# One 512-column matmul for the high weights with both parts of x, in a split-precision projection

## The chip, the cores and the metric

The kernel runs on one core of a Trainium2 chip. The metric is the device time of one execution in microseconds (us), the median of several. Engines are named as in the profile: PE is TensorE's matmul, PEld its weight load, DVE VectorE, ACT ScalarE, POOL GpSimd, SP SyncE, which issues nearly all DMAs.

## The reference

One layer on 256 tokens of width 2048, all in float32. Cut to what matters:

```
hn   = rms_norm(x, attn_norm_g)                      # (256, 2048)
proj = hn @ w_in                                     # 10656 columns
q, k, v      -> differential attention, 8 heads      # 3072 columns, "da"
r, k, v, 416 more columns -> RWKV-7, two scans       # 3488 columns, "rkv" and "lo"
gates = sigmoid(the last 4096 columns)               # "gt"
h = x + (gate_a * (y_a @ w_branch_a) + gate_b * (y_b @ w_branch_b)) @ w_out
out = h + expert_choice_ffn(rms_norm(h))             # 16 experts, 32 tokens each
```

The RWKV columns are mixed with their neighbours in time before use: p + mu * ((prev + next) / 2 - p).

## The kernel before, in words

Every projection of the first half is computed in a split form. A float32 operand a is taken as ah + al, where ah is a rounded to the type float32r and al is the rest; the product is xh·wh + xl·wh + xh·wl, three matmuls into one accumulator. `xh` and `xl` (lines 98 and 99) hold the normalised and transposed input for the whole kernel: 128 partitions, 16 slices of the contraction, 256 tokens. Lines 144 (ACT) and 145 (DVE) fill them.

`wsplit` (line 204) brings a **piece** of weights, 128 x 1024 numbers (512 KB), by one DMA into `raw`; ACT casts it into `wh` (line 211) and DVE subtracts to get `wl` (line 212). Both `wh` and `wl` have two buffers, so the cast of a piece waits until PE has done with the piece two before.

`project_c` (line 236) computes 256 output columns, transposed: two halves of 128 columns, each in its own accumulator (a bank of PSUM; the pool `pj` has two, so each half of the next projection needs the bank of the same half of this one). A projection takes four pieces; a piece serves four slices of the contraction for both halves, that is eight **triples** of matmuls of 256 columns on lines 249, 250 and 251. There are 30 such projections on w_in: 2 for the small RWKV inputs (`lo0`, `lo1`; the second half of `lo1` has 32 columns), 12 for r, k, v (`rkv`) and 16 for the gates (`gt`); with 2 x 16 triples each that makes 960 triples. Two more users of `project_c`, the branch projections (`br`), keep it. The attention inputs (`da`) and the output projection (`wo`) go through `project_t` (line 220), whose three matmuls have 512 columns.

What empties an accumulator before: for `gt`, one ACT activation (line 265) per half; for `rkv` and `lo`, `shift_mix` (line 293), an ACT copy into `prs` (line 296) and an ACT multiplication (line 300), then a POOL addition and a DVE combination.

Four groups of RWKV heads follow one another: `prep`, `invert` (a triangular inverse by 31 steps of small DVE operations, then four copies from PSUM per group, lines 533 to 544) and `chain` (the scan). The order of each engine's instructions is fixed at build time by a list scheduler with priorities: `prep`, `invert` and `chain` have a high one, so have the weights' cast and subtraction (`prio(PS)`) and the `rkv` mixing; the gates have a low one and fill in between (`GSCHED` deals 1, 4, 1, 4 and 6 of them to the groups). Each engine runs its own list strictly in that order.

After the gates come `da`, the attention, the two branch projections, `wo` with the router, and the experts, whose 384 loads of 1 MB of gate, up and down weights run by DMA to the end.

Of the kernel before, what the change touches and what calls it, by code (L numbers as in the profile page):

```python
# [8 lines left out]
F32 = mybir.dt.float32  # L9
F32R = mybir.dt.float32r  # L10
I32 = mybir.dt.int32
AF = mybir.ActivationFunctionType
OP = mybir.AluOpType
# [5 lines left out]
T = 256  # L19
KT = 16  # L20
DA_W = 1024
RW0 = 3 * DA_W
GATE0 = RW0 + 3488
# [29 lines left out]
def trunk_kernel(ctx, tc, x, attn_norm_g, w_in, q_norm_g, k_norm_g, lambda_q1, lambda_k1, lambda_q2,  # L53
# [4 lines left out]
    V, A, G, PE, SP = nc.vector, nc.scalar, nc.gpsimd, nc.tensor, nc.sync  # L58
# [39 lines left out]
    xh = hp.tile([128, KT, T], F32R, name="xh")  # L98
    xl = hp.tile([128, KT, T], F32R, name="xl")
# [117 lines left out]

    w_in_k = w_in[0].rearrange("(kt p) n -> p kt n", p=128)
# [40 lines left out]

    def gates(n):  # L260
        for gt in range(gates_done[0], min(16, gates_done[0] + n)):
            ps = project_c(w_in_k, KT, GATE0 + gt * 256, 256, xh, xl, f"gt{gt}")
            gs = wp.tile([128, 2, T], F32, name="gs", tag="gs", bufs=1)
            for c in range(2):
                A.activation(gs[:, c], ps[c], AF.Tanh, scale=0.5)
            SP.dma_start(gtD[2 * gt:2 * gt + 2].rearrange("c p t -> p c t"), gs)
            gates_done[0] += 1


    with ExitStack() as es:  # L270
# [22 lines left out]
        def shift_mix(ps, m, col, dst):  # L293
            pr = prs[prn[0] % 2]
            prn[0] += 1
            A.copy(pr[:m, 1:T + 1], ps)
            s = r2.tile([128, T], F32, name="shs")
            b = r2.tile([128, T], F32, name="shb")
            last_mix[0] = G.tensor_tensor(s[:m], pr[:m, 0:T], pr[:m, 2:T + 2], op=OP.add)
            A.mul(b[:m], ps, omu[:m, col:col + 1])  # L300
            V.scalar_tensor_tensor(dst, s[:m], prmh[:m, col:col + 1], b[:m], op0=OP.mult, op1=OP.add)
# [31 lines left out]
        ps = project_c(w_in_k, KT, RW0 + 3072, 256, xh, xl, "lo0")  # L333
# [6 lines left out]
        ps = project_c(w_in_k, KT, RW0 + 3328, 160, xh, xl, "lo1")  # L340
# [151 lines left out]
        def invert(G_):  # L492
# [39 lines left out]
            for a_, b_ in ab_:  # L532
                V.tensor_copy(ht[b_], ph[b_])
# [8 lines left out]
            for a_, b_ in ab_:  # L542
                V.tensor_copy(tt[a_, :, 0:4, 32:64], px[a_])
                V.tensor_copy(tt[b_, :, 4:8, 0:32], px[b_])
# [88 lines left out]
        for gp in range(4):  # L633
            rkv = []
            for i in range(3):
                ps = project_c(w_in_k, KT, RW0 + i * 1024 + gp * 256, 256, xh, xl, f"rkv{gp}_{i}")
# [425 lines left out]
```

## Time and profile before

| what | value |
|---|---|
| median of 3 runs | 1839.66 us (1839.43 to 1848.39) |
| the profiled execution's own time | 1838.98 us |
| its span, first to last instruction | 1836.9 us |
| granted TensorE clock, mean | 0.990 of 2.4 GHz |
| PE busy | 1652.7 us (90%), 11083 matmuls |
| DVE, ACT, POOL busy | 701.4, 440.2, 199.2 us |
| DMA queue 1 | 554.41 MB, 81.1% of 16 engines |

The span lies within one execution; 2.1 us more lie around it. Busy times are sums over engine instructions. A matmul's duration includes its way through the array and overlaps the next one's, so the spacing of starts, not the duration, tells how fast a stream of matmuls runs. By stage: up to about 552 us `lo`, `rkv`, `gt` and the RWKV groups; up to 680 us `da`; attention and branches up to 826 us; `wo` and router up to 920 us; experts to the end.

### The profile page before, as it was taken

The page shows a single profiled execution, that of the slowest core. Times are in us where ns is not written, and L with a number is a line of the kernel's source. Part 1 is how long each engine was busy: PE and PEld are TensorE (multiplying, and loading weights), DVE is VectorE, ACT ScalarE, POOL GpSimd, SP SyncE. Part 2 cuts the span into 40 slices and gives each one's busy share as a digit, 9 for nine tenths or more (in the row PEclk, how much of TensorE's full clock was granted, in tenths as well). Part 3 has the DMA queues.
Part 4 walks back from the last instruction along what each step waited for, and adds up shares of the span by engine and source line. Part 5 has one row for each costly group of instructions (what it writes and reads, how often), then busy time and mean ns, then how long its engine had stood idle before and what let it go on. Part 6 is the DMA issues. An engine that isn't in the chain of part 4 may idle for free.

```text
span 1836.9 us, 27260 instructions
## 1 busy us (share of the span) xinstructions
PE 1652.7 (90%) x11083; PEld 1012.1 (55%) x11083; DVE 701.4 (38%) x1520; ACT 440.2 (24%) x766; POOL 199.2 (11%) x308
## 2 busy tenths in 40 slices
PE   6999999999999999999888898888988879888887
PEld 5988988888998778998633332112521115221122
DVE  4687878787746777774410010000100001000001
ACT  5434444443434455444300000000000000000000
POOL 3243223333001321000000000000000000000000
PEclk9999999999999999999989999999999999999999
DMA  6555644456656666789799999999999999999998
GB/s 184 164 141 152 169 120 127 120 139 154 175 141 181 195 209 204 225 271 363 294 390 427 423 420 426 427 427 424 421 425 427 427 425 420 425 426 427 426 420 358
DMA packets 222141, 556.47 MB, mean 303 GB/s; under 512 B 40154, under 2 KB 129104, under 8 KB 188992
## 3 DMA queue, kind: packets, MB, share of 16 engines
q1 hardware_dynamic: 221440, 554.41, 81.1%
q8 instruction: 87, 1.43, 0.3%
q0 software_dynamic: 576, 0.31, 0.2%
q14 instruction: 38, 0.31, 0.1%
HBM read 543.14 MB, written 11.53 MB: 302 GB/s over the span
## 4 chain that ended last, share of the span: by engine, by line
DMA 45%; PE 40%; DVE 7%; POOL 3%; issue 2%; SPq 1%; ACT 1%; DVEq 0%; POOLq 0%; ACTq 0%
DMA w<-in_w_gate_e_dram 22%; DMA w<-in_w_down_e_dram 13%; DMA w<-in_w_up_e_dram 9%; PE pd L982 2%; PE pc_gt L251 2%; PE pc_gt L249 2%; PE pc_gt L250 2%; PE pxe L933 2%; PE pj_da L231 2%; PE pj_da L232 2%; PE pj_da L233 2%; PE pc_rkv L249 2%; PE pc_br L249 2%; PE pc_rkv L251 2%; PE pc_rkv L250 2%
## 5 line engine op out<-in xcount | busy, mean ns | idle before, releaser
L951 PE MATMUL pgu<-w,xe 128*32 128x512 f32 x2048 | 473.9, 600 | 86.4 <-DMA w<-in_w_up_e_dram 44.6
L951 PEld LDWEIGHTS pgu<-w,xe 128*32 128x32 f32 x2048 | 113.7, 109 | 439.8 <-issue 207.3
L982 PE MATMUL pd<-w,hdT 128*32 128x512 f32 x1024 | 217.1, 598 | 32.7 <-DMA w<-in_w_down_e_dram 31.8
L968 DVE SCALAR_TENSOR_TENSOR th<-th,pgu 128x512 f32<-128x512 f32 x8 | 5.5, 688 | 469.4 <-ACT th L967 416.4
L982 PEld LDWEIGHTS pd<-w,hdT 128*32 128x32 f32 x1024 | 54.0, 109 | 182.7 <-issue 90.4
L249 PE MATMUL pc_gt<-xh,wh_gt 128*128 128x256 f32 x512 | 149.1, 294 | 0.0
L251 PE MATMUL pc_gt<-xh,wl_gt 128*128 128x256 f32 x512 | 143.7, 292 | 3.8 <-DVE wl_gt L212 3.5
L250 PE MATMUL pc_gt<-xl,wh_gt 128*128 128x256 f32 x512 | 145.2, 286 | 0.0
L967 ACT ACTIVATE th<-pgu 128x512 f32<-128x512 f32 x8 | 4.8, 598 | 489.8 <-PE pgu L951 489.8
L249 PE MATMUL pc_rkv<-xh,wh_rkv 128*128 128x256 f32 x384 | 112.5, 295 | 2.8 <-ACT shb L300 1.8
L251 PE MATMUL pc_rkv<-xh,wl_rkv 128*128 128x256 f32 x384 | 110.4, 298 | 2.1 <-DVE wl_rkv L212 2.1
L250 PE MATMUL pc_rkv<-xl,wh_rkv 128*128 128x256 f32 x384 | 111.3, 292 | 0.0
L249 PEld LDWEIGHTS pc_gt<-xh,wh_gt 128*128 128x128 f32 x512 | 98.3, 192 | 3.2 <-issue 1.2
L251 PEld LDWEIGHTS pc_gt<-xh,wl_gt 128*128 128x128 f32 x512 | 95.7, 192 | 7.2 <-DVE wl_gt L212 4.8
L250 PEld LDWEIGHTS pc_gt<-xl,wh_gt 128*128 128x128 f32 x512 | 98.5, 192 | 2.0 <-issue 1.3
L212 DVE TENSOR_TENSOR wl_gt<-raw_gt,wh_gt 128x1024 fp32r<-128x1024 f32 x64 | 80.1, 1251 | 31.1 <-ACT wh_gt L211 27.8
L211 ACT CAST wh_gt<-raw_gt 128x1024 fp32r<-128x1024 f32 x64 | 66.9, 1046 | 78.9 <-PE pc_gt L250 64.4
L992 DVE TENSOR_TENSOR acc<-poe,acc 128x512 f32<-128x512 f32 x24 | 16.6, 692 | 175.9 <-PE poe L991 175.9
L987 ACT COPY ye<-pd 128x512 f32<-128x512 f32 x16 | 9.4, 586 | 301.1 <-PE pd L982 301.1
L249 PEld LDWEIGHTS pc_rkv<-xh,wh_rkv 128*128 128x128 f32 x384 | 75.3, 196 | 6.2 <-ACT shb L300 2.6
L232 PE MATMUL pj_da<-wl_da,xh 128*128 128x512 f32 x192 | 76.6, 399 | 1.7 <-DVE wl_da L212 1.7
L251 PEld LDWEIGHTS pc_rkv<-xh,wl_rkv 128*128 128x128 f32 x384 | 73.5, 196 | 5.1 <-DVE wl_rkv L212 2.8
(398 smaller groups left out, 2789.1 us busy)
## 6 DMA issues: line engine op xcount, KB each, us to landing
w<-in_w_gate_e_dram SPq DMA_DIRECT2D x128, 1024.0 KB, 19.6
w<-in_w_up_e_dram SPq DMA_DIRECT2D x128, 1024.0 KB, 19.6
w<-in_w_down_e_dram SPq DMA_DIRECT2D x128, 1024.0 KB, 18.2
raw_gt<-in_w_in_dram SPq DMA_DIRECT2D x64, 512.0 KB, 3.8
raw_rkv<-in_w_in_dram SPq DMA_DIRECT2D x48, 512.0 KB, 3.8
raw_da<-in_w_in_dram SPq DMA_DIRECT2D x48, 512.0 KB, 3.6
raw_wo<-in_w_out_dram SPq DMA_DIRECT2D x32, 512.0 KB, 6.7
raw_br<-in_w_branch_b_dram SPq DMA_DIRECT2D x16, 512.0 KB, 4.7
```

The lines of the kernel that those rows point to most:

```text
L211: cast_ = A.copy(wh[:, :n], raw[:, :n])
L212: low_ = V.tensor_tensor(wl[:, :n], raw[:, :n], wh[:, :n].bitcast(F32), op=OP.subtract)
L231: PE.matmul(ps[t], lh[:, kt, s], wh[:, j], start=first, stop=False)
L232: PE.matmul(ps[t], lh[:, kt, s], wl[:, j], start=False, stop=False)
L233: PE.matmul(ps[t], ll[:, kt, s], wh[:, j], start=False, stop=last)
L249: PE.matmul(ps[c][:m], wh[:, j, cs], rh[:, kt], start=first, stop=False)
L250: PE.matmul(ps[c][:m], wh[:, j, cs], rl[:, kt], start=False, stop=False)
L251: PE.matmul(ps[c][:m], wl[:, j, cs], rh[:, kt], start=False, stop=last)
L933: PE.matmul(px[:, j], h[:, t, kt::KT], ohr[:, t], start=t == 0, stop=t == 1)
L951: PE.matmul(pgu[2 * gu + hf][js], xe[kt // 4][:, kt % 4, js], wt[j][:, k, hf * 512:(hf + 1) * 512], start=kt == 0, stop=kt == KT - 1)
L982: mm = PE.matmul(pd[nb][js], hT[:, ft, js], wf[j], start=ft == 0, stop=ft == 7)
L992: V.tensor_tensor(acc[:, t, cs], po, (h if q == 0 else acc)[:, t, cs], op=OP.add)
```

## The change

`xh` and `xl` become two halves of one tile, side by side for each slice of the contraction. A new `project_w` replaces `project_c` for the 30 projections on w_in: one matmul of 512 columns multiplies the high weights with both (`high`), its result filling a whole bank, xh·wh in the first 256 columns and xl·wh in the last; a matmul of 256 columns adds xh·wl to the first half (`low`). The last slice of a projection runs low before high. A new helper `both` adds the two halves of the bank: ACT copies the second into SBUF, DVE adds the first to it. For the gates the activation then runs once on 512 columns in SBUF; in `shift_mix`, ACT's multiplication reads the sum instead of PSUM. Four copies per group in `invert` go from DVE to ACT.

```diff
-    xh = hp.tile([128, KT, T], F32R, name="xh")
-    xl = hp.tile([128, KT, T], F32R, name="xl")
+    xx_ = hp.tile([128, KT, 2, T], F32R, name="xx_")
+    xh, xl = xx_[:, :, 0], xx_[:, :, 1]
...
+    def project_w(c0, width, name):
+        nct = (width + 127) // 128
+        ps = [pjp.tile([128, 2, T], F32, name=f"pc_{name}_{c}", tag="pj") for c in range(nct)]
+        for kc in range(KT // 4):
+            wh, wl = wsplit(w_in_k[:, 4 * kc:4 * kc + 4, c0:c0 + width], 4, width, f"{name}_{kc}")
+            for c in range(nct):
+                m = min(128, width - c * 128)
+                for j in range(4):
+                    kt = 4 * kc + j
+                    cs = slice(c * 128, c * 128 + m)
+                    high = lambda: PE.matmul(ps[c][:m].rearrange("p a t -> p (a t)"), wh[:, j, cs],
+                                             xx_[:, kt].rearrange("p a t -> p (a t)"), start=kt == 0, stop=kt == KT - 1)
+                    low = lambda: PE.matmul(ps[c][:m, 0], wl[:, j, cs], xh[:, kt], start=False, stop=False)
+                    for f in (high, low) if kt < KT - 1 else (low, high):
+                        f()
+        return ps
...
+    def both(dst, ps):
+        A.copy(dst, ps[:, 1])
+        V.tensor_tensor(dst, ps[:, 0], dst, op=OP.add)
...
-            ps = project_c(w_in_k, KT, GATE0 + gt * 256, 256, xh, xl, f"gt{gt}")
+            ps = project_w(GATE0 + gt * 256, 256, f"gt{gt}")
...
-                A.activation(gs[:, c], ps[c], AF.Tanh, scale=0.5)
+                both(gs[:, c], ps[c])
+            A.activation(gs, gs, AF.Tanh, scale=0.5)
...
-            A.copy(pr[:m, 1:T + 1], ps)
+            both(pr[:m, 1:T + 1], ps)
...
-            A.mul(b[:m], ps, omu[:m, col:col + 1])
+            A.mul(b[:m], pr[:m, 1:T + 1], omu[:m, col:col + 1])
...
-                V.tensor_copy(ht[b_], ph[b_])
+                A.copy(ht[b_], ph[b_])
...
-                V.tensor_copy(tt[a_, :, 0:4, 32:64], px[a_])
-                V.tensor_copy(tt[b_, :, 4:8, 0:32], px[b_])
+                A.copy(tt[a_, :, 0:4, 32:64], px[a_])
+                A.copy(tt[b_, :, 4:8, 0:32], px[b_])
```

The order of instructions moves where one gate projection follows another. The first place is PE's list where the gate projection `pc_gt_..5920` takes over from the one before it (in the name `pc_gt_0` and `pc_gt_1` are the halves, in `wh_gt_0` and `wh_gt_1` the pieces). Before, from the end of piece 0 in the first half:

```order
L251 MATMUL pc_gt_0_5920<-xh,wl_gt_0_5924 128x256
L249 MATMUL pc_gt_0_5920<-xh,wh_gt_1_5953 128x256
L250 MATMUL pc_gt_0_5920<-xl,wh_gt_1_5953 128x256
L249 MATMUL pc_gt_1_5921<-xh,wh_gt_0_5923 128x256
L250 MATMUL pc_gt_1_5921<-xl,wh_gt_0_5923 128x256
L251 MATMUL pc_gt_1_5921<-xh,wl_gt_0_5924 128x256
```

The same place in the changed kernel, whose tile there is `pc_gt_..5930`:

```order
L232 MATMUL pc_gt_0_5930<-xx__82,wl_gt_0_5934 128x256
L230 MATMUL pc_gt_0_5930<-xx__82,wh_gt_1_5955 128x512
L232 MATMUL pc_gt_0_5930<-xx__82,wl_gt_1_5956 128x256
...
L232 MATMUL pc_gt_0_5930<-xx__82,wl_gt_1_5956 128x256
L230 MATMUL pc_gt_1_5931<-xx__82,wh_gt_0_5933 128x512
L232 MATMUL pc_gt_1_5931<-xx__82,wl_gt_0_5934 128x256
```

The second half's first piece, which stood behind one slice's two `wh` products of piece 1, now stands behind all four pairs of piece 1 in the first half, those with `wl` of piece 1 among them. That three or four of these `wl` products stand ahead of the second half's first piece is so at 14 of the 29 changes from one projection to the next, and was at none; with other PE work between at some.

The second place is DVE's list at the same change of projection, in the changed kernel (`wl_gt_1_5956` is the subtraction for the new projection's piece 1, `gs<-pc_gt_1_5834` the added sum that frees the second half's bank of the old one; `tmp`, `xx`, `hng` belong to `invert` and `chain`):

```order
L212 TENSOR_TENSOR wl_gt_1_5956<-raw_gt_1_5954,wh_gt_1_5955 128x1024
L535 TENSOR_TENSOR tmp<-xx,dd 128x16x2
L94 SCALAR_TENSOR_TENSOR hngr<-hng_t,hngr 128x8
L282 TENSOR_TENSOR gs<-pc_gt_1_5834,gs 128x256
L537 TENSOR_TENSOR xx<-xx,tmp 128x16x2
```

The bank is freed behind the subtraction. Before, DVE had no part in freeing it.

The third place is ACT's list there. Before (`gs<-pc_gt` empties the old projection's halves):

```order
L211 CAST wh_gt_0_5923<-raw_gt_0_5922 128x1024
L265 ACTIVATE gs<-pc_gt_0_5794 128x256
L211 CAST wh_gt_1_5953<-raw_gt_1_5952 128x1024
L265 ACTIVATE gs<-pc_gt_1_5795 128x256
```

and in the changed kernel:

```order
L211 CAST wh_gt_0_5933<-raw_gt_0_5932 128x1024
L281 COPY gs<-pc_gt_0_5833 128x256
L211 CAST wh_gt_1_5955<-raw_gt_1_5954 128x1024
L281 COPY gs<-pc_gt_1_5834 128x256
```

ACT's part stands where it stood: the second half's copy comes behind the cast of piece 1.

## Rows read from the trace of the kernel before

**Rows 1.** The page: busy time, and the span in 40 slices of 46 us.

```profile
PE 1652.7 (90%) x11083; PEld 1012.1 (55%) x11083; DVE 701.4 (38%) x1520; ACT 440.2 (24%) x766; POOL 199.2 (11%) x308
...
PE   6999999999999999999888898888988879888887
...
DVE  4687878787746777774410010000100001000001
...
GB/s 184 164 141 152 169 120 127 120 139 154 175 141 181 195 209 204 225 271 363 294 390 427 423 420 426 427 427 424 421 425 427 427 425 420 425 426 427 426 420 358
```

**Rows 2.** Stretches: PE, PEld, DVE, ACT, POOL busy (x instructions), clock, DMA share, GB/s.

```profile
92.00:138.00 46.00, 43.23 (x460) 40.18 (x459) 37.23 (x64) 18.23 (x29) 20.55 (x24) 1.00 0.50 140
184.00:230.00 46.00, 45.17 (x587) 41.47 (x586) 40.58 (x91) 19.67 (x35) 10.77 (x15) 1.00 0.63 167
506.00:552.00 46.00, 46.00 (x533) 42.03 (x532) 18.99 (x25) 17.60 (x30) 4.04 (x8) 1.00 0.48 138
827.00:873.00 46.00, 46.00 (x221) 37.02 (x221) 21.54 (x20) 21.05 (x28) 1.41 (x8) 1.00 0.99 363
```

**Rows 3.** The page: the chain that ended last, share of the span by engine.

```profile
DMA 45%; PE 40%; DVE 7%; POOL 3%; issue 2%; SPq 1%; ACT 1%; DVEq 0%; POOLq 0%; ACTq 0%
```

**Rows 4.** PE's groups by line and shape: count, busy us, mean ns, idle before.

```profile
L249 PE MATMUL pc_gt<-xh,wh_gt 128*128 128x256 f32 x512 | 149.1, 294 | 0.0
...
L249 PE MATMUL pc_rkv<-xh,wh_rkv 128*128 128x256 f32 x384 | 112.5, 295 | 2.8 <-ACT shb L300 1.8 <-ACT wh_rkv L211 0.9
...
L249 PE MATMUL pc_lo<-xh,wh_lo 128*128 128x256 f32 x48 | 14.1, 303 | 0.3 <-ACT xh L144 0.3
...
L249 PE MATMUL pc_lo<-xh,wh_lo 128*32 128x256 f32 x16 | 4.5, 279 | 0.0
```

**Rows 5.** Timeline of PE, gates: two starts, 12 matmuls of 256 columns apart.

```profile
500.11 0.28 PE L251 MATMUL pc_gt<-xh,wl_gt 128*128 128x256 f32 x1
...
501.55 0.28 PE L251 MATMUL pc_gt<-xh,wl_gt 128*128 128x256 f32 x1
```

**Rows 6.** Timeline of PE, `da`: two starts, 7 matmuls of 512 columns apart.

```profile
599.76 0.39 PE L232 MATMUL pj_da<-wl_da,xh 128*128 128x512 f32 x1
...
601.35 0.39 PE L233 MATMUL pj_da<-wh_da,xl 128*128 128x512 f32 x1
```

**Rows 7.** Groups of DVE and ACT by shape: count, busy us, mean ns, idle before.

```profile
L533 DVE COPY ht<-ph 32x512 f32<-32x512 f32 x8 | 5.5, 690 | 2.0 <-PE ph L529 1.9
...
L544 DVE COPY tt<-px 32x256 f32<-32x256 f32 x8 | 3.4, 424 | 0.3
...
L471 DVE TENSOR_TENSOR z<-pz,rkv 128x256 f32<-128x256 f32 x8 | 3.3, 410 | 0.0
...
L265 ACT ACTIVATE gs<-pc_gt 128x256 f32<-128x256 f32 x32 | 12.2, 381 | 14.2 <-PE pc_gt L251 14.0
...
L296 ACT COPY prs<-pc_rkv 128x256 f32<-128x256 f32 x24 | 8.9, 371 | 18.6 <-PE pc_rkv L251 18.6
...
L730 ACT ACTIVATE sqq<-qs 128x512 f32<-128x512 f32 x8 | 5.1, 633 | 0.3
...
L848 ACT COPY hT<-pth 128x512 f32<-128x512 f32 x8 | 4.4, 586 | 0.0
```

**Rows 8.** Timeline, one gate projection taking over from another at 485.08 us.

```profile
484.08 0.38 ACT L265 ACTIVATE gs<-pc_gt 128x256 f32<-128x256 f32 x1 [0.75 <-PE pc_gt L251]
...
485.08 0.28 PE L249 MATMUL pc_gt<-xh,wh_gt 128*128 128x256 f32 x1
485.17 1.05 ACT L211 CAST wh_gt<-raw_gt 128x1024 fp32r<-128x1024 f32 x1 [0.70 <-PE pc_gt L250]
...
486.12 0.38 ACT L265 ACTIVATE gs<-pc_gt 128x256 f32<-128x256 f32 x1
...
486.24 1.23 DVE L212 TENSOR_TENSOR wl_gt<-raw_gt,wh_gt 128x1024 fp32r<-128x1024 f32 x1 [0.79 <-ACT wh_gt L211]
```

**Rows 9.** Who PE waited for up to 560 us: us in total, times, longest.

```profile
PE pprg L116 <- DMA rowg<-in_attn_norm_g_dram: 12.9, 1, 12.9
PE pz L470 <- DVE X L464: 5.0, 3, 1.8
PE pc_gt L251 <- DVE wl_gt L212: 3.5, 4, 1.0
```

More of the change, by code (lines that the diff above doesn't have):

```diff
@@ L332, in trunk_kernel @@
         tc.cur_priority = keep_
-        ps = project_c(w_in_k, KT, RW0 + 3072, 256, xh, xl, "lo0")
+        ps = project_w(RW0 + 3072, 256, "lo0")
         for i, dst in enumerate((thw, adw)):
@@ L339, in trunk_kernel @@
             A.activation(dst[64:128, 1], tl_[64:128], fn)
-        ps = project_c(w_in_k, KT, RW0 + 3328, 160, xh, xl, "lo1")
+        ps = project_w(RW0 + 3328, 160, "lo1")
         for i, m in enumerate((128, 32)):
@@ L635, in trunk_kernel @@
             for i in range(3):
-                ps = project_c(w_in_k, KT, RW0 + i * 1024 + gp * 256, 256, xh, xl, f"rkv{gp}_{i}")
+                ps = project_w(RW0 + i * 1024 + gp * 256, 256, f"rkv{gp}_{i}")
                 dst = r2.tile([128, 2, T], F32, name=f"rkv_{i}", bufs=1)
```

## The prediction

> **What bounds the kernel now.** I read the page first. PE is busy in nearly every slice, DVE is busy to seven or eight tenths in the first dozen slices and hardly at all from the twentieth on, and the transfer rate stands at about 425 GB/s from slice 22 to the end [rows 1]. So there are two halves. The experts are bound by DMA, as the chain of waits says with its 45% for DMA [rows 3]; their first loads fill the DMA engines from about 827 us [rows 2], the last row, so that whatever is won or lost before that point moves the end by the same amount. The change lies wholly in the first 552 us.
>
> The stretches show what rules there [rows 2]. PE is busy for 43 to 46 of 46 us, DVE for 37 to 41 in the stretches with the inverse and for 19 near the end of the gates. The table of waits finds little else: after the 12.9 us of the start, PE's longest sums are 5.0 and 3.5 us [rows 9]. PE is the first bound, DVE a close second between 92 and 414 us. Gates and `rkv` projections are the filler that PE always has, so a shorter filler shortens the stage, unless PE is made to wait.
>
> **What a triple costs, and a pair.** The groups count 512 + 384 + 48 + 16 = 960 triples on w_in [rows 4]. Their means of 279 to 303 ns contain the way through the array, so I take the spacing of starts. Twelve matmuls of 256 columns take 501.55 - 500.11 = 1.44 us, 0.120 us each [rows 5]; seven of 512 take 601.35 - 599.76 = 1.59 us, 0.227 us each [rows 6]. The columns streamed are the same 768 either way; what goes is one fixed share per instruction, 2 x 0.120 - 0.227 = 0.013 us. A triple of 0.360 becomes a pair of 0.347, and 960 of them save 960 x 0.013 = **12.4 us** (with the unrounded 0.0129). No row shows a 512 followed by a 256. At worst the pair costs what the triple does, 0 us saved; at best the 256 hides its fixed share as well, another 0.013 us, 24.8 us saved in all. I take the sum of the two spacings, since each is measured in a stream of its own with a weight load per matmul.
>
> Here a page speaks against the change. The rows make the share that goes 13 ns. The Trainium skill, "TensorE: Matmul & The Clock Gate", section "Back-to-back issue gap", gives columns divided by 2.4 GHz plus 2.5 ns as the isolated spacing: 109 and 216 ns, so that 2.5 ns per triple would go, 2.4 us in all as an estimate. The trace does not agree (120 and 227 ns), and I go by it.
>
> **What emptying a bank costs.** Each of 60 halves gets a DVE addition of a bank's 256 columns and SBUF, 0.410 us by the nearest row, 24.6 us. In return 8 copies of 0.690 and 16 of about 0.42 leave DVE, 12.2 us [rows 7]. DVE has 12.4 us more, in a stage where it has 5 to 9 us to spare in each stretch of 46 [rows 2]: beside PE's work on average, not at every place. ACT: 32 gate activations of 0.381 become 32 copies of 0.371 and 16 activations of 0.633; with the moved copies (8 of at most 0.586, 16 of about 0.37) it has some 20 us more [rows 7], hidden, since it is busy for 18 to 20 us of 46 [rows 2]. The multiplication in `shift_mix` now waits for the sum, which delays `prep` by about half a microsecond per half: it stands behind a whole projection of 11 us for the next operand, and I cost it at nothing; without that cover it would be 24 x 0.4 = 10 us.
>
> Now the path. A bank was free 0.38 us after ACT took it up; now it is ACT's copy and then DVE's addition, 0.371 + 0.410 and some 0.1 us between, about 0.9 us if both are idle. PE needs the first half's bank when the second half has had its last four pairs, 1.39 us later, so a change of projection without other work just fits. At the first change (`lo0` to `lo1`) and where DVE is late it does not; I put **1.5 us** in all, from 0 to 6.
>
> The larger item is the order. One clean change of projection stands in the trace: the next projection starts at 485.08, the cast of its piece 1 at 485.17 (both buffers were taken until then), ACT empties the second half only at 486.12 behind that cast, and the subtraction ends at 486.24 + 1.23 = 487.47, 2.39 us after the start [rows 8]. Before, PE came to that `wl` late, behind both halves of piece 0. In the changed kernel the second half's bank is freed behind cast, copy, subtraction and addition, about 2.9 us after the start, so the scheduler has put piece 1 of the first half ahead of piece 0 of the second, at 14 changes (the order of PE, DVE and ACT above). The first `wl` of piece 1 is then due 4 x 0.347 + 0.227 = 1.62 us after the start; it is there at 2.39, or 2.5, as the last matmul has 512 columns and ends 0.11 us later. PE waits 0.85 us. At five of the 14 nothing else stands between; at the others other PE work covers 0.03 to all of it, which I counted from the order with the spacings above. The sum is **7.5 us**. There is a second wait behind it: the buffer of piece 0 is held until the second half is done with it, and then PE has only piece 1's four pairs and two of piece 2's highs, 1.39 + 0.45 = 1.84 us, until it needs piece 2's `wl`, 2.45 us away: 0.6 us, left whole at three changes and in parts at others, **2.5 us**. If other DVE work delays these subtractions by half a microsecond each time, both grow to 17 us together; if the chain's work that runs on meanwhile saves PE later waits, half of it comes back.
>
> **The sum**, against the profiled execution: 1838.98 - 12.4 + 7.5 + 2.5 + 1.5 = 1838.1, rounded to **1838.0 us**. The median of the three runs shown is 1839.66, 0.7 us above that execution; a difference of 0.5%, 9.2 us, is about what a measurement of this kernel can tell from no change, so below 1830.5 is faster and above 1848.9 slower. The forecast is no difference that can be told.
>
> **The rivals.**
> *The saving arrives.* PE waits at the changes of projection, but the RWKV groups' work runs on then and PE finds its later operands ready; or the 512 gives back more. For it: PE's waits are few before [rows 9], and DVE is busy only 19 of 46 us in the last gates [rows 2], where four of the 14 changes lie. Against it: an in-order PE that waits for `wl` in a stretch of nothing but filler gets nothing back. With 2 us of waits left it gives 1838.98 - 12.4 + 2 = 1828.6 us, faster.
>
> *DVE becomes the bound.* Its place is 92 to 414 us, where it has as little as 5.4 us to spare of 46 [rows 2]. It gets 12.4 us more there, subtractions come later, and the banks hang on it too. The point from which it decides: when the additions find DVE busy so often that its 12.4 us add to the stage, while the waits above grow to 17 us. The time: 1838.98 - 12.4 + 12.4 + 11.5 = 1850.5 us with the waits as summed, up to 1856 with the grown ones, slower. Against it: DVE waits for others too, and idle time between is used by a list scheduler.
>
> *The pair costs as much as the triple.* The columns are the same 768; if the weight load of the 512 cannot hide under the shorter 256, nothing is saved. Then only the waits are left: 1838.98 + 11.5 = 1850.5 us with all of them, 1842 if a third. Against it: weight loads hide at a spacing of 0.120 us now [rows 5]. By the page's 2.5 ns, the saving would be 2.4 us and the time 1848, an estimate near this case; the trace's two spacings speak against that as well.
>
> **How the numbers follow.** The forecast, waits that eat most of the saving, gets 0.50; the saving arrives 0.24; DVE the bound 0.16; pair as triple 0.10, half of it slower and half within. That makes faster 0.25 (with a hundredth from the forecast's lower edge), same 0.54, slower 0.21. The forecast's own range is 1831 to 1846, from a half to one and a half times the 11.5 us of waits and the smaller unknowns. To leave out no more than 2 in 10 it must take in most of the first two rivals: 1827 to 1851 us.
>
> **What would show it.** Right: in the changed profile, starts of pairs 0.347 us apart in a gate stretch; `da` starts within a few microseconds of before; PE's table of waits has new entries at the low matmuls (waiting for DVE's subtraction `wl_gt`, some 5 to 15 us) and the high ones (for the added halves), and the lines of the experts are unchanged. Wrong in size: pairs 0.36 apart (the third rival), or no such waits (the first). Wrong in kind: DVE busy for over 43 of 46 us in the stretches from 92 to 414 us with PE waiting for `prep` and `chain` operands (the second), or a difference that comes after 827 us, which nothing here foresees.

## The result, and the profile after

The changed kernel takes 1852.79 us (median of 7 runs, 1851.10 to 1855.18), the kernel before 1842.18 us (7 runs, 1839.43 to 1848.39): a ratio of 1.0051, 95% interval 1.0038 to 1.0063. It is slower by 10.6 us; the forecast was 1838.0 us, with a range from 1827 to 1851. The profiled executions differ by more, 1851.1 against 1836.9 us of span, since that of before (1838.98 us) lay 3.2 us under its median. The page of the changed kernel, busy time and slices, beside [rows 1]:

```profile
PE 1656.4 (89%) x10123; PEld 951.8 (51%) x10123; DVE 710.3 (38%) x1556; ACT 461.1 (25%) x806; POOL 197.3 (11%) x308
...
PE   6998999989999999999979898888988889888887
...
DVE  4678878797746677875420010000100001000001
...
PEclk9999999999999999999989999999999999999999
```

960 matmuls are gone and PE's busy time has not fallen; DVE has 9 us more. The chain that ended last, beside [rows 3], tells nothing of it:

```profile
DMA 46%; PE 39%; DVE 7%; POOL 2%; issue 2%; SPq 2%; ACT 1%; DVEq 0%; ACTq 0%; POOLq 0%
```

First, where. The first matmul of the branches starts at 710.2 us before and 723.8 after; `wo`, the experts and the end follow 13.9 to 14.2 us later than before. So all of it lies ahead of the branches, and behind them nothing changed, as predicted. The stretches, first those of [rows 2] in the changed kernel:

```profile
92.00:138.00 46.00, 42.85 (x303) 34.54 (x302) 34.48 (x63) 19.19 (x30) 17.25 (x21) 0.96 0.49 141
184.00:230.00 46.00, 41.56 (x412) 33.94 (x413) 39.07 (x88) 22.90 (x40) 12.54 (x16) 1.00 0.60 164
506.00:552.00 46.00, 43.87 (x514) 35.72 (x513) 19.21 (x25) 23.09 (x44) 4.97 (x8) 1.00 0.61 165
827.00:873.00 46.00, 46.00 (x230) 38.25 (x229) 23.81 (x24) 20.22 (x24) 1.22 (x7) 1.00 0.91 328
```

In the first two, DVE is no busier than it was (34.5 and 39.1 us, before 37.2 and 40.6), but PE is idle for 4.4 us of 46 in the second, where it was idle for 0.8. Now three long stretches (the same columns), the kernel before:

```profile
46.00:552.00 506.00, 483.15 (x5423) 446.52 (x5421) 381.25 (x837) 215.81 (x377) 135.87 (x185) 0.99 0.54 145
552.00:598.00 46.00, 44.86 (x209) 36.78 (x208) 29.67 (x60) 19.98 (x23) 8.75 (x14) 1.00 0.62 183
```

and the changed one:

```profile
46.00:552.00 506.00, 469.21 (x4384) 381.23 (x4383) 382.54 (x862) 232.76 (x411) 133.93 (x185) 0.98 0.53 142
552.00:598.00 46.00, 45.48 (x288) 36.39 (x287) 27.05 (x55) 19.36 (x24) 0.00 (x0) 1.00 0.55 161
```

PE was idle for 506 - 483.15 = 22.9 us between 46 and 552, and is for 36.8: **13.9 us more**. The granted clock fell to its lower level five times up to the branches, and does eight times, 3.41 us each (each fall takes 0.04 off the clock of a stretch of 46 us); half of that is lost, 8.5 us before and 13.6 after: **5.1 us more**. That holds for these two executions. Over the executions on record with their clock, its mean is 0.9886 for the kernel before (87 of them, from 0.985 at some 1846 us to 0.993 at 1839) and 0.9874 for the change (7), a difference of some 2 us: part of the 5.1 is the spread between executions.

Whom PE waits for, 46 to 552 us (in total, times, longest), beside [rows 9]:

```profile
PE pc_gt L232 <- DVE wl_gt L212: 6.7, 9, 2.3
PE psn L621 <- DVE uu L617: 4.4, 2, 3.3
PE pc_gt L230 <- DVE prs L282: 3.9, 1, 3.9
PE ph L554 <- DVE tst L544: 3.3, 2, 2.5
...
PE pc_gt L230 <- DVE gs L282: 2.7, 3, 1.7
PE pc_rkv L232 <- DVE wl_rkv L212: 2.2, 2, 1.8
PE pc_gt L230 <- DVE pp__4524 L447: 2.0, 1, 2.0
```

Added up over the whole list: low matmuls 9.6 us (before, L251: 5.8), high ones 10.3 (before, L249 and L250: 2.7; of the 10.3, 7.6 are waits for the added halves, `prs` and `gs`), the RWKV groups' products 16.3 (before 13.9). One place shows the new wait and what it draws after it. DVE, then ACT, then PE:

```profile
149.89 1.21 DVE L212 TENSOR_TENSOR wl_gt<-raw_gt,wh_gt 128x1024 fp32r<-128x1024 f32 x1
157.98 0.22 DVE L535 TENSOR_TENSOR tmp<-xx,dd 128x62 f32<-128x62 f32 x1 [6.89 <-DMA dd<-scn]
...
158.89 0.42 DVE L282 TENSOR_TENSOR prs<-pc_rkv,prs 128x256 f32<-128x256 f32 x1
```
```profile
152.71 0.37 ACT L281 COPY prs<-pc_rkv 128x256 f32<-128x256 f32 x1 [0.53 <-PE pc_rkv L230]
152.98 1.05 ACT L211 CAST wh_gt<-raw_gt 128x1024 fp32r<-128x1024 f32 x1
159.35 0.51 ACT L325 ACTIVATE shb<-prs,omu 128x256 f32<-128x256 f32 x1 [5.32 <-DVE prs L282]
```
```profile
159.37 0.79 PE L230 MATMUL pc_gt<-xx__82,wh_gt 128*128 128x512 f32 x1 [3.86 <-DVE prs L282]
...
160.17 0.63 PE L230 MATMUL pc_gt<-xx__82,wh_gt 128*128 128x512 f32 x1
160.60 0.41 PE L232 MATMUL pc_gt<-xx__82,wl_gt 128*128 128x256 f32 x1
160.81 0.63 PE L230 MATMUL pc_gt<-xx__82,wh_gt 128*128 128x512 f32 x1
```

ACT had copied its halves of both banks by 153.1 us. The addition stands in DVE's list behind the inverse's first step, and that waits 6.89 us for its DMA, with DVE idle. The bank stays taken, PE stands for 3.86 us, ACT's multiplication for 5.32. Then the clock is at its lower level, and pairs run 0.64 us apart instead of 0.35. Two stretches there show it; the clock is the number behind the five engines:

```profile
155.50:159.10 3.60, 0.01 (x1) 0.00 (x0) 1.01 (x5) 0.00 (x0) 0.00 (x0) 0.99 1.05 287
159.10:162.50 3.40, 3.13 (x9) 2.67 (x10) 3.30 (x8) 2.83 (x8) 1.88 (x3) 0.51 0.03 11
```

DVE's waits for that DMA in all (up to 560 us), before and in the changed kernel:

```profile
DVE tmp L510 <- DMA dd<-scn: 15.3, 4, 5.6
```
```profile
DVE tmp L535 <- DMA dd<-scn: 25.1, 4, 8.7
```

Undisturbed, seven pairs take 552.65 - 550.21 = 2.44 us, 0.349 each; before, three matmuls took 0.360 [rows 5].

```profile
550.21 0.40 PE L230 MATMUL pc_gt<-xx__82,wh_gt 128*128 128x512 f32 x1
...
552.65 0.39 PE L230 MATMUL pc_gt<-xx__82,wh_gt 128*128 128x512 f32 x1
```

Over all pairs the median spacing is 0.233 us from a 512 to the 256 and 0.117 back, 0.350, so the pairs gave 9.6 to 10.9 us. The account up to the branches is -9.6 + 13.9 + 5.1 = +9.4 us of the 13.6; the 4.2 us that are left are not accounted for.

### The profile page after: what moved, and what is told of

Same layout as the page of the kernel before. It is cut to its first block, busy times and chain, and to the rows that moved or that the text cites. A ratio compares the mean times of both kernels' runs of the same rounds, so it can differ in the third digit from the quotient of the medians.

```text
span 1851.1 us, 25423 instructions
## 1 busy us (share of the span) xinstructions
PE 1656.4 (89%) x10123; PEld 951.8 (51%) x10123; DVE 710.3 (38%) x1556; ACT 461.1 (25%) x806; POOL 197.3 (11%) x308
## 4 chain that ended last, share of the span: by engine, by line
DMA 46%; PE 39%; DVE 7%; POOL 2%; issue 2%; SPq 2%; ACT 1%; DVEq 0%; ACTq 0%; POOLq 0%
DMA w<-in_w_gate_e_dram 22%; DMA w<-in_w_down_e_dram 12%; DMA w<-in_w_up_e_dram 8%; PE pc_gt L230 4%; PE pc_rkv L230 3%; PE pd L1007 2%; PE pc_gt L232 2%; PE pxe L958 2%; PE pj_da L250 2%; PE pj_da L251 2%; PE pj_da L252 2%; PE pc_rkv L232 2%; PE pc_br L268 2%; PE pc_br L270 2%; PE pc_br L269 2%
## 5 line engine op out<-in xcount | busy, mean ns | idle before, releaser
L1007 PE MATMUL pd<-w,hdT 128*32 128x512 f32 x1024 | 219.1, 598 | 31.2 <-DMA w<-in_w_down_e_dram 30.2
L230 PE MATMUL pc_gt<-xx__82,wh_gt 128*128 128x512 f32 x512 | 188.1, 410 | 9.4 <-DVE prs L282 3.9
L232 PE MATMUL pc_gt<-xx__82,wl_gt 128*128 128x256 f32 x512 | 141.9, 293 | 7.4 <-DVE wl_gt L212 6.7
L230 PE MATMUL pc_rkv<-xx__82,wh_rkv 128*128 128x512 f32 x384 | 141.6, 411 | 1.0 <-DVE prs L282 1.0
L230 PEld LDWEIGHTS pc_gt<-xx__82,wh_gt 128*128 128x128 f32 x512 | 95.3, 191 | 30.4 <-DVE prs L282 4.4
L232 PE MATMUL pc_rkv<-xx__82,wl_rkv 128*128 128x256 f32 x384 | 106.1, 293 | 2.4 <-DVE wl_rkv L212 2.2
L232 PEld LDWEIGHTS pc_gt<-xx__82,wl_gt 128*128 128x128 f32 x512 | 98.2, 192 | 17.3 <-DVE wl_gt L212 10.5
L230 PEld LDWEIGHTS pc_rkv<-xx__82,wh_rkv 128*128 128x128 f32 x384 | 71.5, 191 | 17.1 <-DVE prs L282 2.3
L232 PEld LDWEIGHTS pc_rkv<-xx__82,wl_rkv 128*128 128x128 f32 x384 | 73.7, 192 | 10.6 <-DVE wl_rkv L212 4.7
L251 PE MATMUL pj_da<-wl_da,xx__82 128*128 128x512 f32 x192 | 77.3, 403 | 1.9 <-DVE wl_da L212 1.9
L252 PE MATMUL pj_da<-wh_da,xx__82 128*128 128x512 f32 x192 | 75.1, 391 | 0.0
L250 PE MATMUL pj_da<-wh_da,xx__82 128*128 128x512 f32 x192 | 70.1, 401 | 0.0
```

The source lines that it names most:

```text
L230: high = lambda: PE.matmul(ps[c][:m].rearrange("p a t -> p (a t)"), wh[:, j, cs], xx_[:, kt].rearrange("p a t -> p (a t)"), start=kt == 0, ...
L232: low = lambda: PE.matmul(ps[c][:m, 0], wl[:, j, cs], xh[:, kt], start=False, stop=False)
L250: PE.matmul(ps[t], lh[:, kt, s], wh[:, j], start=first, stop=False)
L251: PE.matmul(ps[t], lh[:, kt, s], wl[:, j], start=False, stop=False)
L252: PE.matmul(ps[t], ll[:, kt, s], wh[:, j], start=False, stop=last)
L1007: mm = PE.matmul(pd[nb][js], hT[:, ft, js], wf[j], start=ft == 0, stop=ft == 7)
```

## The experiments

Each kernel was compared with runs of the kernel before on the same chip; each theory is told in the expectation that first names it; a ratio has its 95% interval. The time is the median. The stages below come from one traced execution each, which can lie a few us off the median (before 3.2 under it, e12 4.1 over): the end of the last gate projection, the end of `pg` (the last product of the last group's `chain`), how many of the 576 `da` matmuls ran ahead of it, and the start of the branches, us.

| kernel | time, us | ratio to before | gates end | last `pg` | `da` ahead | branches | from `pg` |
|---|---|---|---|---|---|---|---|
| before | - | 1 | 552.4 | 563.7 | 36 | 710.2 | 146.5 |
| changed | 1852.8 | 1.0051 | 562.5 | 590.5 | 96 | 723.8 | 133.3 |
| e1 no addition | 1844.2 | 1.0006 | 542.1 | 582.0 | 96 | 717.6 | 135.6 |
| e2 triples, two engines | 1869.7 | 1.0149 | 586.6 | 580.8 | 0 | 743.2 | 162.4 |
| e3 halves in turn | 1861.1 | 1.0098 | 550.0 | 597.5 | 96 | 732.8 | 135.3 |
| e5 before, halves in turn | 1851.7 | 1.0053 | 563.5 | 574.8 | 36 | 721.2 | 146.4 |
| e7 triples, ACT moves | 1841.9 | 0.9996 | 557.7 | 565.4 | 24 | 714.5 | 149.1 |
| e8 e1, inverse on DVE | 1855.5 | 1.0063 | 546.0 | 593.2 | 96 | 727.3 | 134.1 |
| e9 three buffers | 1882.0 | 1.0206 | 560.8 | 605.7 | 96 | 729.7 | 124.0 |
| e10 before, three buffers | 1859.1 | 1.0080 | 559.0 | 581.1 | 80 | 708.1 | 127.0 |
| e11 ACT empties | 1852.8 | 1.0055 | 552.2 | 592.8 | 96 | 726.8 | 134.0 |
| e12 gates only | 1848.6 | 1.0035 | 562.7 | 590.7 | 96 | 724.1 | 133.4 |
| e13 rkv only | 1845.5 | 1.0014 | 558.0 | 572.8 | 48 | 716.5 | 143.7 |
| e14 gate sum first | 1853.9 | 1.0062 | 548.8 | 589.4 | 96 | 723.3 | 133.9 |
| e15 e11, gates late | 1858.7 | 1.0088 | 566.7 | 595.9 | 96 | 729.5 | 133.6 |
| e16 before, gates late | 1841.3 | 0.9988 | 553.7 | 561.4 | 24 | 710.4 | 149.1 |
| e17 gates late | 1845.8 | 1.0018 | 558.4 | 586.4 | 96 | 719.8 | 133.4 |
| e18 triples at the end | 1851.2 | 1.0052 | 563.8 | 578.6 | 48 | 722.3 | 143.7 |
| e19 e11, POOL adds | 1870.4 | 1.0148 | 579.0 | 604.2 | 84 | 739.8 | 135.5 |
| e20 e1, gates late | 1844.7 | 1.0002 | 542.7 | 583.3 | 96 | 717.1 | 133.8 |

### What the addition costs, and what the pairs save without it

**e1** empties a bank with one ACT copy of its first half (the product xl·wh is computed, but left out of the result).

```diff
-        A.copy(dst, ps[:, 1])
-        V.tensor_tensor(dst, ps[:, 0], dst, op=OP.add)
+        A.copy(dst, ps[:, 0])
```

> The change, but each bank's first half is copied to SBUF by ACT alone: no DVE addition, so the xl*wh term is left out of all 30 projections' results (the matmuls that make it still run). Theory 1 (the pair saves some 9 us, emptying a bank by two engines and the order that follows from it cost some 20): 1831 to 1836 us, ratio to before about 0.995, and PE's waits for DVE at the high matmuls gone. Theory 2 (DVE's 12 us more are what is paid): DVE now has less work than before, so the same 1831 to 1836. Theory 3 (the pair saves nothing): 1840 to 1844, as before.

Measured: 1844.18 us, ratio 1.0006 (0.9994 to 1.0018), against 1831 to 1836 by theories 1 and 2. So the additions, with the waits that hang on them, cost 0.45%, some 8 us, and without them the time is that of the kernel before, though a pair is shorter than a triple. Its stretches:

```profile
46.00:552.00 506.00, 482.60 (x4455) 394.31 (x4453) 374.52 (x811) 239.87 (x420) 135.42 (x185) 0.98 0.55 148
552.00:598.00 46.00, 38.89 (x233) 29.81 (x233) 25.59 (x63) 13.45 (x17) 8.12 (x14) 0.93 0.37 109
```

PE's idle time up to 552 us is back at before's (23.4 us) and the gates end 10.3 us sooner. But behind them PE is idle for 7.1 us of 46 and its clock falls twice (before, it is idle for 1.1 us there and the clock does not fall): 6.0 us more of idle time and 3.4 of clock, about what the pairs had saved. Who it waits for there:

```profile
PE hngpb L399 <- DVE hngsq L396: 3.0, 1, 3.0
PE pj_da L251 <- DVE wl_da L212: 2.6, 1, 2.6
PE hngps L387 <- ACT hngsq L384: 1.5, 1, 1.5
```

These are the last steps of the last group's chain: nothing is left to put between them.

**e7** is the kernel before with the rest of the change but no pairs: one ACT copy empties a bank, the gate activation runs once from SBUF, the inverse's copies are on ACT. **e2** is the same with the bank emptied by two engines.

```diff
 def both(dst, ps):      # ps: the triples' one sum
+    A.copy(dst, ps)                                                    # e7
+    A.mul(dst, ps, 0.5)                                                # e2
+    V.scalar_tensor_tensor(dst, ps, 0.5, dst, op0=OP.mult, op1=OP.add) # e2
```

> Triples of before, each half emptied by one ACT copy (no DVE addition), the gates' activation on 512 columns in SBUF, the inverse's copies on ACT: the change's moves on ACT alone. Theory A (shorter pieces on PE lay bare the path of cast and subtraction): as before, 1840 to 1846 us. Theory B (the work moved to ACT costs about 10 us, which hid the pairs' gain in the run without the addition): 1850 to 1858 us.

> The triples of before, in 256 columns, but with everything else of the change: each half is emptied by an ACT copy (of one half of the value) and a DVE operation that adds the other half, the activation runs on SBUF, the inverse's copies are on ACT. Theory 1: slower than the change by what the pair saves, 1858 to 1864 us. Theory 3: the same as the change, 1850 to 1855.

Measured: e7 0.9996 (0.9985 to 1.0006), as theory A had it; e2 1.0149 (1.0130 to 1.0168), 1869.7 us and above both of its theories. The moves to ACT cost nothing by themselves. With one engine per bank, pairs take 1844.2 - 1841.9 = 2.3 us more than triples, which the two intervals do not tell from nothing, and not 9.6 less; with two engines they take 17 less. So the second engine costs triples 28 us and pairs 9.

**e8** is e1 with the inverse's copies back on DVE (the last hunk of the diff undone).

> Pairs with an ACT copy of the first half alone (xl*wh left out of the results of the 30 projections), the inverse's copies on DVE as before. Theory A: no better than with the copies on ACT, 1840 to 1846 us. Theory B: the pairs' gain shows, 1830 to 1836 us.

Measured: 1855.49 us, 1.0063 (1.0050 to 1.0076), 11 us above e1 and above both theories. The copies on ACT help the pairs; and `pg` is 11 us later for 16 + 8 copies, 12 us of work, on another engine of the groups' path.

### Is it the handing over of banks?

**e3** lays the pieces of w_in differently: eight slices for one half, not four for both, so that a bank has 16 pairs of slack. **e5** does the same to the kernel before.

```diff
-        for kc in range(KT // 4):
-            wh, wl = wsplit(w_in_k[:, 4 * kc:4 * kc + 4, c0:c0 + width], 4, width, ...)
-            for c in range(nct):
+        for c in range(nct):
+            for kc in range(KT // 8):
+                wh, wl = wsplit(w_in_k[:, 8 * kc:8 * kc + 8, c0 + c * 128:c0 + c * 128 + m], 8, m, ...)
```

> The change with another order of the weights: a piece holds 8 slices of 128 columns instead of 4 of 256, so one half of a projection is finished before the other begins and a bank has 16 pairs (5.6 us) to be emptied instead of 4 (1.4 us). DVE and ACT have the same work as in the change; DMA rows are 512 bytes instead of 1024. Theory 1: the waits at the changes of projection go, 1832 to 1838 us, faster than before. Theory 2: DVE's work is the same, so 1848 to 1854, as the change.

> The kernel before (triples, emptied as before) with the pieces of 8 slices of 128 columns: the control of the run with the halves in turn. Theory 1: no handover waits to win back, so 1838 to 1844 us, as before. If the 512-byte rows of the DMA cost something, it shows here as slower than before, at most 10 us.

Measured: e3 1.0098 (1.0078 to 1.0117), above both theories; e5 1.0053 (1.0036 to 1.0069), 8 us slower, as its last clause allowed. The pieces cost something by themselves; against e5 the pairs lose 9.4 us, nearly as much as without slack, although from 46 to 552 us no high matmul of e3 waits for an added half any more. The handover as the whole cause does not stand.

**e11** frees a bank by ACT alone; DVE adds from SBUF. **e14** puts the gates' copy and addition at the priority of the cast and the subtraction.

```diff
+        A.copy(hv[:m], ps[:, 0])
-        V.tensor_tensor(dst, ps[:, 0], dst, op=OP.add)
+        V.tensor_tensor(dst, hv[:m], dst, op=OP.add)      # e11
...
+                with prio(PS):                            # e14
                     both(gs[:, c], ps[c])
```

> The change, but ACT copies both halves of a bank to SBUF and DVE adds them there, so that a bank is free as soon as ACT has been at it twice and never waits for DVE. Theory S (the additions stand in DVE's list behind operations that wait for a DMA or for PE, the bank stays taken, PE's high matmuls wait some 11 us in all and the clock falls more often, 13.6 against 8.5 us lost): the waits at the high matmuls go to under 3 us and the time falls by about 10, to 1843. Theory P (the RWKV groups' own path has become longer, because the scheduler now puts more filler columns between two steps of the scan, 28 matmul widths of 256 where 23 stood): the waits at the high matmuls go as well, but the gates then end some 10 us earlier, the last chain still ends at 585 us or later, PE waits and loses its clock there, and the time stays at 1850 to 1856.

> The change with the gates' copy and addition at the high priority that the cast and the subtraction have. Theory S: the bank is freed sooner, the waits at the gates' high matmuls (8 us or so) go, 1845. Theory P: the additions go ahead of the groups' own DVE steps, so the chain is no sooner: 1852 to 1857.

Measured: e11 1852.76 us, 1.0055 (1.0040 to 1.0069); e14 1853.94 us, 1.0062 (1.0046 to 1.0078). Both times are as theory P said. Whom e11's high matmuls wait for, 46 to 552 us, all there is:

```profile
PE pc_gt L230 <- ACT wh_gt L211: 2.2, 1, 2.2
PE pc_rkv L230 <- ACT shb L285: 1.0, 1, 1.0
```

The waits for additions are gone, PE's idle time up to 552 us fell from 36.8 to 31.2 us and the gates end 10 us sooner than in the change. Then this:

```profile
552.00:598.00 46.00, 41.47 (x284) 31.85 (x284) 23.77 (x64) 14.89 (x22) 0.49 (x2) 0.93 0.43 125
```

4.0 us more idle time than the change has there, and the clock at its lower level for 6.8 us. What is won at the banks is lost behind the gates.

e14 tests less than was meant: its high matmuls wait 10.0 us, nearly as long as in the change (10.3), so the banks came no sooner and theory S was not put to the test there. The longest of these waits:

```profile
PE pc_gt L230 <- DVE prs L282: 5.9, 3, 3.8
PE pc_gt L230 <- DVE gs L282: 2.8, 3, 1.5
```

Its gates do end 13.7 us sooner than in the change, at 548.8 us, but `pg` comes no more than 1.1 us sooner, and nothing is won.

**e19** is e11 with the additions on POOL (`G.tensor_tensor`).

> The kernel in which ACT empties both halves of a bank, with the additions from SBUF on POOL in place of DVE. If DVE's 24 us of additions hold the groups up (theory D): PE's idle time from 46 to 552 us falls from 31 us to about 24, as in the kernel without additions, and the time to 1843 to 1847. If ACT's extra copies or the order of the pairs alone do it: no change, 1850 to 1855. POOL's own steps (0.5 to 1.4 us, in the chain as well) may come later; above 1855 that takes more than DVE gains.

Measured: 1870.40 us, 1.0148 (1.0132 to 1.0164), a miss: 18 us more. PE's idle time from 46 to 552 us is 47.9 us. An addition takes POOL 0.84 to 0.86 us where DVE took 0.45 to 0.47 in e11, and DVE's waits for POOL's steps `z` and `sw` up to 552 us grew from 11.1 us in the change to 20.8, as the last clause had it; whether DVE gained, the run can't tell.

### Is it the stream of weights?

**e9** and **e10** give `wh` and `wl` a third buffer, with 15 instead of 16 tiles for the experts' weights to make room, in the changed kernel and in before.

```diff
-NEW, NE1, NEB = 16, 2, (6, 2)
+NEW, NE1, NEB = 15, 2, (6, 2)
...
-        wh = wp.tile([128, 1024], F32R, name="wh_" + name, tag="wh")
+        wh = wp.tile([128, 1024], F32R, name="wh_" + name, tag="wh", bufs=3)   # wl too
```

> The change with three buffers each for the high and the low weights instead of two, so that cast and subtraction of a piece need not wait for the piece two before; paid for in SBUF by one expert tile less fetched ahead (15 instead of 16). Theory A: the projections' waits for the subtraction go, 1838 to 1846 us, 7 to 14 below the change. Theory B, or the bank's emptying as the cause: 1850 to 1856 us.

> The kernel before with the same three buffers and 15 tiles ahead: the control. Theory A: it had 0.1 us more per piece, so little to win, 1837 to 1844 us. If the control falls as much as the change does, the third buffer helps any kernel here and says nothing of the pair.

Measured: e9 1882.01 us, 1.0206 (1.0192 to 1.0221); e10 1859.09 us, 1.0080 (1.0067 to 1.0092). Both are above all that was expected. The pairs lose 23 us against their control: a third buffer does not bring the saving. But the run does more than it was meant to. From 46 to 552 us the low matmuls wait only 0.5 us for `wl`, and the waits of the high ones for the added halves have grown from 7.6 us to 21.1, most of it in this line:

```profile
PE pc_gt L230 <- DVE gs L282: 15.4, 8, 4.7
```

So the wait moved to the banks, and e9 can't show that two buffers cost the change nothing. Nor do its time and e10's measure the buffers alone: e10 starts its branches 2 us sooner than the kernel before, and from there to the end both take some 21 us longer than their counterparts with 16 tiles.

### Where the pairs stand: gates or rkv

**e12** keeps pairs and additions for the gates alone, **e13** for `lo` and `rkv` alone (the other projections go through `project_c` and are emptied as before).

> Pairs and added halves for the 16 gates alone; lo0, lo1 and the 12 rkv projections as before with triples, one ACT copy and the multiplication from the bank. Theory S: the rkv banks' waits and the later sum in the mixing go, the gates' stay: about two thirds of the loss, 1849. Theory P: prep and the first groups run as before up to the first gates, but the scans stand among pairs as in the change: 1848 to 1853, and 28 widths between two steps as in the change.

> Pairs and added halves for lo0, lo1 and rkv alone; the gates as before with triples and the activation from the bank. Theory S: a third of the loss stays, some 1845. Theory P: the scans stand among the gates' triples again, 23 widths between two steps, the last chain ends within 5 us of before (562 us) and the time is 1838 to 1843.

Measured: e12 1.0035 (1.0022 to 1.0048), e13 1.0014 (1.0004 to 1.0024). Two thirds of the loss come with the gates. Both are where theory S had them, and e13 is above what P gave it; but e11 had spoken against S, and what differs in the traces is the last scan. In each of its rounds the products `prr`, `pu` and `psn` follow one another, each needing what came of the one before. The last round, the starts of its products in PE's timeline; before:

```profile
528.31 0.69 PE L575 MATMUL prr<-su,X 128*64 128x64 f32 x16
...
531.62 0.68 PE L590 MATMUL pu<-rh,tt 64*64 64x64 f32 x16
...
534.96 0.69 PE L596 MATMUL psn<-uu,bt 128*64 128x64 f32 x16
...
539.00 0.69 PE L575 MATMUL prr<-su,X 128*64 128x64 f32 x16
```

and in the changed kernel:

```profile
543.68 0.69 PE L600 MATMUL prr<-su,X 128*64 128x64 f32 x16
...
547.30 0.68 PE L615 MATMUL pu<-rh,tt 64*64 64x64 f32 x16
...
554.01 0.69 PE L621 MATMUL psn<-uu,bt 128*64 128x64 f32 x16
...
558.79 0.69 PE L600 MATMUL prr<-su,X 128*64 128x64 f32 x16
```

This round takes 15.1 us instead of 10.7 (the one ahead of it 11.2 instead of 12.3), and PE is never idle in it: gate matmuls stand between. It is not a late operand either; `psn` at 554.01 needs the second half of `uu`:

```profile
550.08 0.43 DVE L617 COPY uu<-pu 64x256 f32<-64x256 f32 x1
```

That was there at 550.5, 3.5 us sooner. The list scheduler has put more columns between two steps: counted in widths of 256, from `psn` to `prr` 15, 28 and 29 in the scan's three rounds where 23, 24 and 22 stood, and from `pu` to `psn` 45, 34 and 47 where 26, 29 and 19 stood. From the end of the inverse's last product to the start of the last `pm` behind the scan it is 55.4 us, before 48.2, in e1, e11, e12 and e14 58 to 60, in e13 46.0. Why the scheduler does so for pairs can't be read from a trace. And the scan is the smaller part: the inverse's last product ends at 518.2 us, before at 502.5, so 15.7 of the 26.8 us by which the last `pg` is later had come up ahead of it. No run singles out what delays the inverse.

### Does the last chain bound the time?

**e18** is the change with triples, emptied as before, in gates 10 to 15 alone. **e17** is the change, **e15** e11, **e16** the kernel before and **e20** e1 with one gate moved from ahead of the last `rkv` to the end.

```diff
-GSCHED = (1, 4, 1, 4, 6)
+GSCHED = (1, 4, 0, 4, 7)
```

> The change, but gates 10 to 15 as before (triples, activation from the bank), so that only the last scan stands among triples. Theory P: 23 widths between two of its steps in place of 28, 46 to 49 us from the inverse's last product to the norm in place of 55, the last norm ends near 581 and the time is 1844 to 1848. If the pairs among the earlier groups or the banks are what costs, the time stays above 1850.

Measured: 1851.20 us, 1.0052 (1.0038 to 1.0066), a miss for theory P, and the time that the expectation's last clause gave to the other causes. The scan did as P expected: it takes 46.0 us and `pg` ends at 578.6, 12 us sooner than in the change, although the inverse's last product ends as late, at 518.0. But the gates still end at 563.8 us, with 36.1 us of idle time up to 552, and PE has no idle time from 552 to 598: by the trace PE's work is then the bound, and it is as late as in the change.

> The change itself with the same move. Theory P: the path to the last norm starts sooner (579 instead of 589), but the waits at the banks keep the gates until about 560, so less is won than with ACT emptying: 1845 to 1850. Theory S: no change, 1852 to 1855.

> The kernel in which ACT empties both halves of a bank, with one gate moved from ahead of the last rkv projections to the end (1, 4, 0, 4, 7). Theory P: the last rkv projection ends about 10 us sooner, near 367, the path behind it is as long as before (some 212 us to the last norm), so the norm ends near 579 instead of 589, the gates still end near 552, and the time falls to 1842 to 1846. Theory S or any theory in which PE's work and its waits at the projections bound the stage: no change, 1851 to 1855.

> Control: the kernel before with the same move of one gate. Theory P: there the gates already last until 10 us before the last norm, so nothing is won; within 4 us of the kernel before, rather slower, as group 2 has less filler. If this kernel gains as much as the one with pairs, the move has nothing to do with the pairs.

> Pairs with the product of the low part of x left out and no addition, with one gate moved from ahead of the last rkv projections to the end (1, 4, 0, 4, 7). Theory of the tail: PE's idle time from 552 to 598 us falls from 7 us to about 2 and its clock stays, the norm of the last group ends sooner than 579, and the time is 1835 to 1839, faster than before by most of the pairs' saving. If the tail is not what takes the saving: 1842 to 1846, as without the move.

Measured: e17 1845.84 us, 1.0018 (1.0009 to 1.0027), a hit; e15 1858.73 us, 1.0088 (1.0074 to 1.0102), 6 us the other way; e16 1841.28 us, 0.9988 (0.9978 to 0.9998), rather faster where rather slower was expected; e20 1844.74 us, 1.0002 (0.9991 to 1.0012), no change. In e17, e20 and e16 the last `rkv` projection ended 14 to 37 us sooner (in e15 only 0.7), and in e20 `pg` came no sooner (583.3 us, e1 582.0): that projection is not what holds the last group, and on this point P was wrong. By the ratios, one gate moved is worth -6 to +6 us through the order that it gives. Effects of that size in a single kernel say little, those of e12 and e13 among them, and the 8 us of e1 are not far above.

The table's last columns suggest what holds it all together. In all kernels with pairs in every gate but e19, **exactly 96** `da` matmuls ran ahead of `pg`: one block of the six. Block 1 takes its banks from the chain's own pool (`(chp, "ch") if blk in (1, 3)` in the loop over the blocks), so PE has 96 x 0.227 = 21.8 us of other work behind the gates and no more until the chain is done, and the branches start 133 to 136 us behind `pg` (e9, with other buffers, 124). The last `pg` products before, then in the changed kernel, and one line of the `da` products that ran there up to 590 us (32 each on L250, L251 and L252):

```profile
L628 PE MATMUL pg<-sgd,g2b x4: 379/379/379, 562.3 to 563.3; 128*128 128x256 f32 x4
```
```profile
L653 PE MATMUL pg<-sgd,g2b x4: 379/379/379, 589.0 to 590.1; 128*128 128x256 f32 x4
...
L252 PE MATMUL pj_da<-wh_da,xx__82 x32: 387/389/397, 563.6 to 587.9; 128*128 128x512 f32 x32
```

The rest is read from the traces and not shown by a run. In e1 this work has run out before `pg`, PE idles, and the end of the chain sets the time; in the changed kernel it ends just with `pg`, PE being busy for 45.5 of 46 us, and both bounds lie at the same place. No run gave block 1 other banks, so that it would help was not tried; nor was e1 with triples among the last scan, which by the two bounds should be the fastest.

## Why the prediction was wrong

Two steps failed: the price of emptying a bank, put at 1.5 us, and the claim that a shorter filler shortens the stage. Term by term:

- *The base.* The sum starts from one execution, 1838.98 us, 3.2 us under the median of seven; from the median it gives 1841.3. That is a fifth of the miss.
- *The pairs, 12.4 us.* Nearly right: 0.349 to 0.350 us a pair, not 0.347; 9.6 to 10.9 us. By the isolated spacing of the Trainium skill, "TensorE: Matmul & The Clock Gate", section "Back-to-back issue gap", 2.4 us would have gone, an estimate from its 2.5 ns per matmul. The trace does not agree: 10 to 11 ns went per triple.
- *The waits for `wl`, 7.5 + 2.5 us.* The kind was right, the size not: 9.6 us at L232 against 5.8 at L251 before, 3.8 more. Why it was less than summed, no run shows.
- *Emptying banks, 1.5 us.* Failed: 10.3 us at the high matmuls against 2.7, 7.6 more. I compared durations with slack, 0.9 us against 1.39, as if DVE took the addition when it came. It takes it in its list's order, behind steps that wait for something else: for `dd` alone DVE waits 25.1 us (before 15.3), and the 3.86 us at 159 us are such a place.
- *"Beside PE's work on average", and the mixing's later sum at nothing.* Failed as well. DVE had the time on average, but the groups' own steps stand in the same lists: the groups' products wait 2.4 us more, and e1, which takes the additions out, gains 8 us. e11 takes their hold on the banks away, at the price of a second ACT copy, and gains nothing: freeing the banks sooner is not enough.
- *The clock.* Not in the sum at all: 5.1 us in the two profiled executions, some 2 on the average of all.
- *"Gates and `rkv` are the filler that PE always has, so a shorter filler shortens the stage."* False at the end of the stage, and the deeper error: even without additions (e1) the gates end 10.3 us sooner and the time is no better, since the last chain ends 18 us later than before with only one block of `da` to cover it. That the block is what binds is read from the traces; what delays the chain stays open. I read PE's 46.00 busy of 46 near the end of the gates [rows 2] as a bound and did not ask how soon behind it another one stood: 11 us, the last `pg` at 563.7.
- *The rivals.* The time came out in the second one's interval (1850.5 to 1856 us), but not by its sign: DVE is busy for 33 to 40 us of 46 from 92 to 414 us, not 43. DVE's load alone is not the bound. How much of the loss is the place of the additions in DVE's list and how much the 25 us that they take, no run separates. That the pair would cost as much as the triple fell by its spacing; `da` starting within a few microseconds of before was wrong (563.0 against 552.3), and that nothing changes behind 827 us was right.

The total of new waits, 11.5 us in the sum and 13.9 measured, was close by luck: it was made of other waits.

## What to carry to other kernels

Where in-order engines share the emptying of a bank with a latency-bound chain, cost an added instruction by what stands ahead of it in its list, waits included, not by the engine's spare time. Before crediting a shorter filler, look up when the chain that it covers ends and what may run behind it: here one block of 21.8 us, by the traces held there by a pool of banks. And where a scheduler orders by its own costs, compare the spacing of the chain's steps in both traces first, as PE without idle time can still run them late.

No kernel with pairs beat the kernel before; the only kernel that did beyond its interval is e16, the kernel before with one gate moved, by 0.12% (0.02 to 0.22).

## What was not expected of the hardware

After a stand of PE of 3.86 us the granted clock was at 1.2 GHz (0.51 of full speed) for 3.4 us although matmuls came without a pause again, and 256 and 512 columns took 0.21 and 0.43 us from start to start. And in the mixed stream a 512 gives the following 256 0.233 us, 0.006 more than between 512s [rows 6], and a 256 the following 512 only 0.117, 0.003 less than between 256s [rows 5]: nearly the sum of the two streams, as forecast.
